# Hybrid DeltaNet and Conformer layer on one core: gates as seven half-size products ahead of the heads, branch products token-major, the mixed sum turned on TensorE

## The chip, the core and the metric

The kernel runs on one core of a Trainium2 chip. The metric is the device time of one execution in microseconds. The kernel before takes 2469.19 us, the median of 3 runs (2468.35 to 2469.48).

The engines have short names in the profile: PE is TensorE (matmul), PEld its weight load, DVE is VectorE, ACT ScalarE, POOL GpSimd, SP SyncE, which here only issues DMAs. L186 is line 186 of the kernel before.

## The reference, cut to what matters

512 tokens, 2048 channels, float32 throughout.

```
h = rmsnorm(x)
qkv, z_a, b_raw, a_raw, glu_in, z_b, gate_logits = split(h @ w_in)
o_a = gated_delta(short_conv(qkv), b_raw, a_raw)         # 16 heads, chunks of 64
y_a = (rmsnorm(o_a) * silu(z_a)) @ w_br_a                # branch A
u   = causal_depthwise_conv(glu(glu_in), 31 taps) + b_dw
y_b = (silu(layernorm(u)) * silu(z_b)) @ w_br_b          # branch B
gate_a, gate_b = split(sigmoid(gate_logits + b_gate))
mixed = (gate_a * y_a + gate_b * y_b) @ w_out
x = x + rmsnorm(mixed)
x = x + rmsnorm(sigmoid(x @ w_ple_gate) * (p @ w_ple_proj))
```

## The kernel before

**Numbers.** Every float32 factor is split into a high part, rounded to the type fp32r, and a low part, the rest. A product is three matmuls: high by high, high by low, low by high. ScalarE makes the high part of a weight piece (L127, a cast) and VectorE the low part (L128, a subtraction of two SBUF tensors). A piece is 128x512; `prep` makes two of them from one 512 KB load on SP's queue, and `next_piece` keeps three ahead in a ring of four buffers.

**Products.** `gemm_cm` (L170) makes one channel-major tile: 128 channels by 512 tokens, the weights stationary, 16 steps of the inner dimension with three matmuls each, so 48 matmuls and four pieces a tile. Its results take turns in two PSUM banks (the pool `gps`); an `evac` function empties each. z_a (in `z_phase`) and `w_out` are made another way, as seven half-size products (Strassen's scheme in Winograd's form) with 128x512 matmuls and the activations stationary: 336 matmuls for half of the 2048 columns where the plain way has 384. The sums of activations that it needs are formed once by the generator `form`, the sums of weight blocks by VectorE (the helper line L314) and by a DMA that adds (`acc`, on GpSimd's queue). For `w_out` these sums are made ahead by `presum` (L980): 160 DMAs on GpSimd's queue, 96 of them loads (L992), 64 stores (L997).

**Order.** The kernel is a list of jobs in program order. After each matmul of a job, `tick()` moves the generators that are active: the heads' chain (`group`, a step every HP = 4 matmuls), the depthwise convolutions (`dwconv`, one of their 30 VectorE steps every CP = 6), `presum`, `layer_norm`, and `mix`, which forms the sums of activations for `w_out`. The framework then puts the instructions of each engine in an order of its own: it follows the program order, but work that it takes to be ready may be put ahead into an engine's idle time. Each engine runs its list in order.

The stages, with their time in the trace:
- loading and normalising x, with the part of the layer embedding that doesn't depend on x1 (to 36 us)
- 5 gate tiles, then z_a as seven products (to 250 us), then the decay inputs
- the 16 heads in 8 groups of 2 (to 1191 us): per group 6 tiles of q, k, v, then `spawn(group)`, then 2 of the `rest` tiles (z_b and gates); after the last group 4 more rest tiles and the first GLU pair. `finish("heads")` issues what is left of the chain
- branch A (to about 1850 us): 16 tiles of `w_br_a`, among them the other 15 GLU pairs and the other gate tiles, with the convolutions on VectorE (L924: u and the running sum y both in SBUF) and `presum`. GpSimd adds up the channels for the layer norm (L930, two SBUF tensors)
- the layer norm of branch B's convolution, behind the remaining gate tiles; then 16 tiles of `w_br_b` (to 2119 us), with the `mix` steps
- `w_out`, 14 half-size products; the layer embedding's gate; the output (to 2467 us)

The gates go to DRAM (`g_dram`) and come back for branch A (L976, multiplied with the product from PSUM) and branch B (L1107, L1109).

Of the kernel before, what the change touches and what calls it, by code (L numbers as in the profile page):

```python
# [27 lines left out]
CP = 6  # L28
# [5 lines left out]
GATE_TILE0 = 113  # L34
# [5 lines left out]
V_BG = V_DW + NK * TAPS  # L40
V_BDW = V_BG + 32
# [41 lines left out]
def _body(ctx, tc, A, out):  # L83
# [31 lines left out]
    prepped = deque()  # L115

    def prep():
        if not prep_src:
            return
        src = prep_src.popleft()  # L120
        raw = rawp.tile([P, 1024], F32, tag="raw", name="raw", bufs=3)
        nc.sync.dma_start(raw, src)
        for q in range(2):
            rq = raw[:, q * T:(q + 1) * T]
            w = ring.tile([P, 1024], F32R, tag="w", name="w")
            hi, lo = w[:, 0:T], w[:, T:]
            nc.scalar.copy(hi, rq)  # L127
            nc.vector.tensor_tensor(lo, rq, hi.bitcast(F32), ALU.subtract)  # L128
            hi_lo[id(hi)] = w.rearrange("p (s c) -> p s c", s=2)
            prepped.append((hi, lo))  # L130
# [138 lines left out]
    g_dram = dram.tile([2 * NK, P, T], F32, name="g_dram")  # L269
    zb_dram = dram.tile([NK, P, T], F32, name="zb_dram")  # L270

    def gate_tile(i, src=True):
        def f(ps):
            t = slots.tile([P, T], F32, tag="s", name="gt")
            nc.scalar.activation(t, ps, AF.Sigmoid, bias=vv(V_BG + i))
            nc.sync.dma_start(g_dram[i], t)
        gemm_cm(w_in_tile(GATE_TILE0 + i) if src else None, hT, f)

    def zb_tile(i):
# [4 lines left out]
        gemm_cm(w_in_tile(ZB_TILE0 + i), hT, f)  # L284

    first_src = [w_in_tile(GATE_TILE0)[0], w_in_tile(GATE_TILE0)[1]]
# [20 lines left out]
    def z_phase():  # L307
# [49 lines left out]
        WZ = A["w_z"]  # L357
# [4 lines left out]
        def load(jp, blk, q):  # L362
            cnt["load"] += 1
            if cnt["load"] <= 4 or cnt["load"] % 5 in (2, 4):
                two = [slots.tile([P, T], F32, tag="s", name="zraw") for _ in range(2)]
                for n in range(2):
                    nc.sync.dma_start(two[n], WZ[jp, blk, q][:, n * T:(n + 1) * T])
                return two
            raw = rawp.tile([P, 1024], F32, tag="raw", name="raw", bufs=3)
            nc.sync.dma_start(raw, WZ[jp, blk, q])  # L370
            return [raw[:, 0:T], raw[:, T:]]

        def acc(t, jp, blk, q):
            nc.gpsimd.dma_start(t, WZ[jp, blk, q], accum_op=ALU.add)

# [3 lines left out]
        def e_a(jp, q):  # L379
            b11, b12 = load(jp, B11, q), load(jp, B12, q)  # L380
# [6 lines left out]
        def e_b(jp, q):  # L387
            b22, b12 = load(jp, B22, q), load(jp, B12, q)
# [6 lines left out]
        def e_c(jp, q):  # L395
            acc(tz[q], jp, B21, q)
            return [load(jp, B21, q), parts(tz[q])]

        for jp in range(2):
            for e in (e_a, e_b, e_c):  # L400
                entries.extend((e, jp, q) for q in range(4))

        def enter():
            e, jp, q = entries.popleft()
            for src in e(jp, q):
# [36 lines left out]
        def fin(tt, j, c):  # L442
# [4 lines left out]

        gen = form()
        gate_tile(0, False)
        for i in range(1, FILL):  # L450
            if i == FILL - 1:
                jobs.extend([enter, enter])
            gate_tile(i)
        spawn(gen, 7, "form")
        run_jobs()
        for jp in range(2):
            ps = run(("P1", "Q5"), stepper(gen, 2))
            s1, s5 = [], []
            for home, pr in ((s1, "P1"), (s5, "Q5")):
                for t in range(2):  # L460
                    home.append(unit_s("zsn"))
                    nc.scalar.copy(home[t], ps[pr][t])
# [7 lines left out]
            for t in range(2):  # L470
                tt_(d[t], ps["P3"][t], d[t], ALU.add)
                fin(t, 2 * jp + 1, d[t])
                tt_(s5[t], s5[t], u2[t], ALU.subtract)
                fin(2 + t, 2 * jp + 1, s5[t])
            ps = run(("P2", "Q4"))
            for t in range(2):
                tt_(s1[t], ps["P2"][t], s1[t], ALU.add)
                fin(t, 2 * jp, s1[t])
                tt_(u2[t], ps["Q4"][t], u2[t], ALU.add)
                fin(2 + t, 2 * jp, u2[t])  # L480
# [266 lines left out]
    def group(g):  # L747
# [134 lines left out]
        while scans:  # L882
            wait = None
            for s in list(scans):
# [3 lines left out]
                else:  # L888
# [3 lines left out]
    rest = deque([lambda i=i: zb_tile(i) for i in range(NK)] + [lambda i=i: gate_tile(i) for i in range(FILL, NK)]  # L892
                 + [lambda i=i: gate_tile(NK + i) for i in range(NK)])
    for g in range(NH // 2):
        pair = (2 * g, 2 * g + 1)
        for h in pair:
            gemm_cm(w_in_tile(16 + h), hT, evac_k(h))
            gemm_cm(w_in_tile(h), hT, evac_q(h))
            gemm_cm(w_in_tile(32 + h), hT, evac_v(h))
        jobs.append(lambda g=g: spawn(group(g), HP, "heads"))  # L900
        for _ in range(2):
            rest.popleft()()


# [4 lines left out]
    cpool = [slots, "s"]  # L909

# [22 lines left out]

    def evac_glu_a(i):
        def f(ps):
            u = sg_t.pop(i)
            nc.vector.tensor_tensor(u, ps, u, ALU.mult)
            spawn(dwconv(i, u), CP)
        return f

    def glu_pair(i):
        gemm_cm(w_in_tile(GLU_TILE0 + 16 + i), hT, evac_glu_b(i))
        gemm_cm(w_in_tile(GLU_TILE0 + i), hT, evac_glu_a(i))

    mixed = [None] * NK
    gate_b = [None] * NK

    for i in range(4):
        rest.popleft()()
    glu_pair(0)  # L950
    run_jobs()
    finish("heads")
    heads_ctx.close()


    s2_ctx = ExitStack()
    lop = s2_ctx.enter_context(tc.tile_pool(name="lop", bufs=LOP))
    s2 = s2_ctx.enter_context(tc.tile_pool(name="s2", bufs=40 - LOP))
    cpool[:] = [s2, "s2"]

    def low(n, name, dt=F32R):
        return lop.tile([P, T], dt, tag="lop", name=name) if n < LOP else s2.tile([P, T], dt, tag="s2", name=name)
    oT = []

    def split_oa():
        for h in range(NH):
            oh = low(2 * h, "oh")
            nc.scalar.copy(oh, o_a[h])
            ol = low(2 * h + 1, "ol")
            nc.vector.tensor_tensor(ol, o_a[h], oh.bitcast(F32), ALU.subtract)  # L970
            oT.append((oh, ol))
            yield
    spawn(split_oa(), 7, "oa")
    def evac_ya(i):
        def f(ps):
            nc.vector.tensor_tensor(mixed[i], ps, mixed[i], ALU.mult)  # L976
        return f

# [4 lines left out]

# [29 lines left out]
    def load_gate(i):  # L1013
        mixed[i] = slots.tile([P, T], F32, tag="s", name="gt")
        nc.sync.dma_start(mixed[i], g_dram[i])

    rest.popleft()()
    glu_pair(1)
    jobs.append(lambda: finish("oa"))
    for i in range(3):  # L1020
        jobs.append(lambda i=i: load_gate(i))
    jobs.append(lambda: spawn(presum(), 10, "presum"))
    nglu = 2
    for i in range(NK):
        gemm_cm(A["w_br_a"][i], oT, evac_ya(i))
        if i + 3 < NK:
            jobs.append(lambda i=i: load_gate(i + 3))
        if i + 5 < NK:
            rest.popleft()()
        if nglu < NK:  # L1030
            glu_pair(nglu)
            nglu += 1
# [5 lines left out]

    def layer_norm():
        while done[0] < NK:  # L1040
            yield
        for i in range(NK):
            u_t[i] = s2.tile([P, T], F32, tag="s2", name="ur")
            nc.sync.dma_start(u_t[i], u_dram[i])
            yield 3
        pm = lps.tile([P, T], F32, tag="l", name="mean_ps")
        mm(pm, ones, acc[0], start=True, stop=True)
        mean = low(0, "mean", F32)
        nc.vector.tensor_scalar(mean, pm, 1.0 / D, None, ALU.mult)
        acc2 = low(0, "acc2", F32)  # L1050
        for i in range(NK):
            u = u_t[i]
            nc.vector.tensor_tensor(u, u, mean, ALU.subtract)
            sq = low(0, "lsq", F32) if i else acc2
# [3 lines left out]
            yield 12  # L1058
        yield
        pvr = lps.tile([P, T], F32, tag="l", name="var_ps")  # L1060
        for tt in range(NTT):
            mm(pvr[:, tt:tt + 1], acc2[:, tt * P:(tt + 1) * P], ones[:, 0:1], start=True, stop=True)
        yield
# [4 lines left out]
        dg = low(0, "dg", F32)  # L1068
        for tt in range(NTT):
            nc.vector.tensor_scalar(dg[:, tt * P:(tt + 1) * P], ident, rst[:, tt:tt + 1], None, ALU.mult)  # L1070
        yield
        yield
        prs = lps.tile([P, T], F32, tag="l", name="rstd_ps")
        mm(prs, ones, dg, start=True, stop=True)
        rstd = low(0, "rstd", F32)
# [508 lines left out]
```

## Time and profile before

| what | before |
|---|---|
| runs, median of 3 | 2469.19 us |
| profiled execution: span from the first to the last instruction | 2467.1 us |
| instructions | 33147 |
| POOL busy | 219.0 us (9%) |
| ACT busy | 1110.7 us (45%) |
| HBM read, written | 310.90 MB, 48.23 MB |

The profiled execution's time outside the span isn't recorded; the median of the runs is 2.1 us above the span. Busy times of PE overlap: a 128x512 matmul is shown as some 0.39 us, but matmuls start every 0.23 us when nothing holds them up, so PE's cost is read from how many start in a stretch, not from the mean.

### The profile page before, as it was taken

How to read it: one execution, taken by the hardware profiler on the slowest of the kernel's cores; microseconds unless marked ns; L12 is line 12 of the kernel's file. 1: busy time of each engine (PE TensorE's matmuls, PEld its weight loads, DVE VectorE, ACT ScalarE, POOL GpSimd, SP SyncE). 2: the span in 40 equal slices, each digit the busy share in tenths (PEclk: the TensorE clock that was granted, in tenths of full speed). 3: DMA queues.
4: the chain of work that ended last, by engine and by line, in shares of the span. 5: the costliest groups of instructions: out<-in, count | busy, mean ns of one | idle time of the engine just before them, and what ended most of it. 6: DMA issues, size and time to landing. Idle time of an engine off the chain costs nothing.

```text
span 2467.1 us, 33147 instructions
## 1 busy us (share of the span) xinstructions
PE 2446.8 (99%) x12090; PEld 2014.3 (82%) x12090; DVE 1746.4 (71%) x3278; ACT 1110.7 (45%) x2181; POOL 219.0 (9%) x291
## 2 busy tenths in 40 slices
PE   8999999999999999999999999999999999999998
PEld 7888788888888888888888888888888888888886
DVE  7877767767676776766886877868976755667644
ACT  6455565565645556564422222222224723444532
POOL 0001100100000000000222322310000000000000
PEclk9999999999999999999999999999999999999999
DMA  7566432323232232223676866853353633575542
GB/s 268 171 173 187 133 110 86 99 86 99 74 103 95 82 99 86 98 69 115 181 224 179 235 204 181 239 161 111 106 185 123 210 118 109 213 234 168 196 171 77
DMA packets 131460, 361.31 MB, mean 146 GB/s; under 512 B 14816, under 2 KB 23264, under 8 KB 131296
## 3 DMA queue, kind: packets, MB, share of 16 engines
q1 hardware_dynamic: 112096, 310.94, 37.8%
q0 software_dynamic: 18048, 46.15, 8.1%
q10 hardware_dynamic: 1152, 2.10, 0.3%
q8 instruction: 95, 1.56, 0.3%
q14 instruction: 69, 0.57, 0.1%
HBM read 310.90 MB, written 48.23 MB: 146 GB/s over the span
## 4 chain that ended last, share of the span: by engine, by line
PE 96%; DVE 1%; issue 1%; DMA 1%; ACT 1%; POOL 0%; SPq 0%; DVEq 0%; POOLq 0%; ACTq 0%
PE g L186 23%; PE g L188 23%; PE g L184 23%; PE zp L434 2%; PE zp L432 2%; PE zp L433 2%; PE f L1274 2%; PE f L1273 2%; PE f L1272 2%; PE f L1438 2%; PE f L1436 2%; PE f L1437 2%; PE psB L704 1%; PE psS L710 1%; PE psA L698 1%
## 5 line engine op out<-in xcount | busy, mean ns | idle before, releaser
L186 PE MATMUL g<-hl,w 128*128 128x512 f32 x2048 | 809.2, 395 | 0.0
L188 PE MATMUL g<-hh,w 128*128 128x512 f32 x2048 | 809.0, 395 | 0.0
L184 PE MATMUL g<-hh,w 128*128 128x512 f32 x2048 | 807.5, 394 | 0.0
L127 ACT CAST w<-raw 128x512 fp32r<-128x512 f32 x716 | 438.3, 619 | 728.6 <-PE g L188 620.0
L128 DVE TENSOR_TENSOR w<-raw,w 128x512 fp32r<-128x512 f32 x716 | 504.2, 709 | 275.4 <-ACT w L127 273.0
L188 PEld LDWEIGHTS g<-hh,w 128*128 128x128 f32 x2048 | 385.1, 188 | 76.2 <-DVE w L128 2.6
L186 PEld LDWEIGHTS g<-hl,w 128*128 128x128 f32 x2048 | 385.1, 188 | 76.1 <-issue 1.6
L184 PEld LDWEIGHTS g<-hh,w 128*128 128x128 f32 x2048 | 385.2, 188 | 74.1 <-issue 0.5
L924 DVE SCALAR_TENSOR_TENSOR uc<-sg,vec,uc 128x511 f32<-128x511 f32 (+14 forms) x480 | 351.3, 734 | 14.0 <-ACT uc L921 3.9
L651 DVE SCALAR_TENSOR_TENSOR cv<-g,vec,cv 128x511 f32<-128x511 f32 x144 | 106.4, 739 | 28.5 <-ACT cv L649 27.8
L184 PE MATMUL g<-oh,w 128*128 128x512 f32 x256 | 99.6, 389 | 0.0
L186 PE MATMUL g<-ol,w 128*128 128x512 f32 x256 | 99.6, 389 | 0.0
L188 PE MATMUL g<-oh,w 128*128 128x512 f32 x256 | 99.6, 389 | 0.0
L184 PE MATMUL g<-uh,w 128*128 128x512 f32 x256 | 99.6, 389 | 0.0
L186 PE MATMUL g<-ul,w 128*128 128x512 f32 x256 | 99.6, 389 | 0.0
L188 PE MATMUL g<-uh,w 128*128 128x512 f32 x256 | 99.6, 389 | 0.0
L837 DVE TENSOR_TENSOR prod<-UT,VT 128x2 f32<-128x2 f32 (+30 forms) x248 | 87.3, 352 | 6.6
L992 POOL DMA_DIRECT2D wsum<-in_w_out x96 | 75.3, 847 | 78.1 <-issue 28.1
L1272 PE MATMUL f<-wsp,oph 128*128 128x512 f32 x192 | 75.6, 394 | 0.0
L1436 PE MATMUL f<-w,xh 128*128 128x512 f32 x192 | 75.3, 392 | 0.0
L1273 PE MATMUL f<-wsp,opl 128*128 128x512 f32 x192 | 75.3, 392 | 0.0
L1274 PE MATMUL f<-wsp,oph 128*128 128x512 f32 x192 | 75.2, 392 | 0.0
(370 smaller groups left out, 3406.6 us busy)
## 6 DMA issues: line engine op xcount, KB each, us to landing
raw<-in_w_in SPq DMA_DIRECT2D x258, 512.0 KB, 3.3
wsum<-in_w_out POOLq DMA_DIRECT2D x96, 256.0 KB, 5.8
raw<-in_w_ple_gate SPq DMA_DIRECT2D x40, 512.0 KB, 3.4
raw<-in_w_br_a SPq DMA_DIRECT2D x32, 512.0 KB, 3.8
wo_sums<-wsum POOLq DMA_DIRECT2D x64, 256.0 KB, 4.2
raw<-in_w_br_b SPq DMA_DIRECT2D x32, 512.0 KB, 3.3
raw<-in_w_z SPq DMA_DIRECT2D x22, 512.0 KB, 4.4
rw<-wo_sums SPq DMA_DIRECT2D x20, 512.0 KB, 4.2
```

What stands on the lines that cost most here:

```text
L127: nc.scalar.copy(hi, rq)
L128: nc.vector.tensor_tensor(lo, rq, hi.bitcast(F32), ALU.subtract)
L184: mm(ps, wh, rh, start=(k == 0), stop=False)
L186: mm(ps, wh, rl, start=False, stop=False)
L188: mm(ps, wl, rh, start=False, stop=(k == NK - 1))
L651: nc.vector.scalar_tensor_tensor(y[:, s:], ps[:, 0:T - s], vv(w0 + 3 - s), y[:, s:], ALU.mult, ALU.add)
L837: pin(nc.vector.tensor_tensor(pv_, um, vm, ALU.mult))
L924: nc.vector.scalar_tensor_tensor(y[:, s:], u[:, 0:T - s], vv(w0 + TAPS - 1 - s), y[:, s:], ALU.mult, ALU.add)
L1272: mm(ps, lh, wh[:, c], start=kk == 0, stop=False)
L1273: mm(ps, ll, wh[:, c], start=False, stop=False)
L1274: mm(ps, lh, wl[:, c], start=False, stop=kk == 7)
L1436: mm(ps[tt], lh, wh, start=k == 0, stop=False)
```

## The change

- **Gates.** `z_phase` runs over three weight matrices instead of one: z_a, the gates of branch A, the gates of branch B (two halves each). The bias comes as a broadcast row on ScalarE's queue and is added as the first two products leave PSUM. The 32 gate tiles are gone; the five tiles that open the stage are z_b tiles now.
- **Heads.** The rest tiles are the other 11 z_b tiles and the first 2 GLU pairs (15 tiles, so the last group gets one), and after the last group come 3 GLU pairs. `presum` starts behind the first group, a step every 13 matmuls instead of 10. `finish("heads")` comes 336 matmuls after the last `spawn(group)` instead of 384.
- **Convolutions.** One generator, `convs`, takes them one after the other, a step every 4 matmuls. It starts behind the last group. From GLU pair 5 on, u lies in PSUM (the pool `ups`, two banks); for pairs 0 to 4 it lies in SBUF as before.
- **Branch A.** `branch` makes token-major strips (512 tokens by 512 channels, four PSUM banks, the activations stationary), in 16 quarter strips of 48 matmuls. After pair 5 each of the pairs 6 to 15 is followed by one quarter strip; six are left for the layer norm. From the end of the heads to the layer norm's mean, GpSimd makes the low parts of the weight pieces (`low_part`).
- **Layer norm and branch B.** Mean and 1/std stay in PSUM. Branch B begins when two of the 16 normalised tiles are there, and `wanted` issues the rest as its steps need them. The strips come in the order 0, 2, 1, 3.
- **Mixed sum.** The sum is token-major now; `turned` brings it back to channel-major by four 128x128 transposes for each of the 16 tiles.
- **`w_out`.** Its products come in the order P1, P7 of the first half, P1 of the second, then the others.

```
-            nc.vector.tensor_tensor(lo, rq, hi.bitcast(F32), ALU.subtract)
+            low_part[0].tensor_tensor(lo, rq, hi.bitcast(F32), ALU.subtract)
...
-        for jp in range(2):
+        for grp, jp in [(g, n) for g in WZ for n in range(2)]:
+            rows = None if grp == "z" else bias_rows(grp, jp)
             ps = run(("P1", "Q5"), stepper(gen, 2))
...
-                    nc.scalar.copy(home[t], ps[pr][t])
+                    if rows:
+                        tt_(home[t], ps[pr][t], rows[n], ALU.add)
+                    else:
+                        nc.scalar.copy(home[t], ps[pr][t])
...
+    def convs():
+        while done[0] < NK:
+            if waiting:
+                yield from dwconv(*waiting.popleft())
+            else:
+                yield
...
-            u = sg_t.pop(i)
-            nc.vector.tensor_tensor(u, ps, u, ALU.mult)
-            spawn(dwconv(i, u), CP)
+            sg = sg_t.pop(i)
+            u = ups.tile([P, T], F32, tag="u", name="up") if ups else sg
+            nc.vector.tensor_tensor(u, ps, sg, ALU.mult)
+            waiting.append((i, u))
...
+        if g == 0:
+            jobs.append(lambda: spawn(presum(), 13, "presum"))
+        for _ in range(2):
+            if rest:
+                rest.popleft()()
...
+    jobs.append(lambda: spawn(convs(), CP, "convs"))
+    for i in range(2, 5):
+        glu_pair(i)
+    run_jobs()
+    finish("heads")
...
+    low_part[0] = nc.gpsimd
...
+    def branch(W, j, q, lhs, evac, side=None):
+        prep_src.extend([W[j, 2 * q], W[j, 2 * q + 1]])
+
+        def job():
+            if q == 0:
+                branch_ps[j] = [yps.tile([P, T], F32, tag="y", name="yp") for _ in range(NTT)]
+            ps = branch_ps[j]
+            for k in range(4 * q, 4 * q + 4):
+                wh, wl = next_piece()
+                if side:
+                    side(k)
+                for tt in range(NTT):
+                    b = slice(tt * P, (tt + 1) * P)
+                    lh, ll = lhs[k]
+                    mm(ps[tt], lh[:, b], wh, start=k == 0, stop=False)
...
+    glu_pair(5)
     jobs.append(lambda: finish("oa"))
+    for i in range(6, NK):
+        glu_pair(i)
+        next_ya()
...
     def layer_norm():
-        while done[0] < NK:
-            yield
         for i in range(NK):
+            while done[0] <= i:
+                yield
...
+        low_part[0] = nc.vector
+        pm = ups.tile([P, T], F32, tag="u", name="sum_ps")
         mm(pm, ones, acc[0], start=True, stop=True)
...
+            yield 6
...
+    jobs.append(lambda: spawn(norm, 4, "norm"))
+    while ya:
+        next_ya()
...
+    def turned(kk):
+        ps = gps.tile([P, T], F32, tag="g", name="tp")
+        for tt in range(NTT):
+            c = (kk % 4) * P
+            nc.tensor.transpose(ps[:, tt * P:(tt + 1) * P], mixed[tt][kk // 4][:, c:c + P], ident)
+        return ps
...
+    def wanted(k):
+        while uT[min(k + 1, NK - 1)] is None:
+            next(norm)
```

373 lines of the change are left out of this document (191 added, 182 removed).

## The prediction, put down before the change was run

> **What bounds the kernel now.** I read the page first: the busy shares, the slices, the chain that ended last.
>
> ```profile
> PE 2446.8 (99%) x12090; PEld 2014.3 (82%) x12090; DVE 1746.4 (71%) x3278; ACT 1110.7 (45%) x2181; POOL 219.0 (9%) x291
> PE   8999999999999999999999999999999999999998
> DVE  7877767767676776766886877868976755667644
> PE 96%; DVE 1%; issue 1%; DMA 1%; ACT 1%; POOL 0%; SPq 0%; DVEq 0%; POOLq 0%; ACTq 0%
> ```
>
> PE is busy in all slices but the first and the last, and the chain is PE for 96% of the span. The view of cores and PE's waits ask whether PE is slowed or waits:
>
> ```profile
> core 0: 2467.1 us, clock 0.999
> PE e_ps L216 <- ACT w L127: 6.1, 1, 6.1
> PE zp L434 <- DVE zw L314: 0.5, 1, 0.5
> PE zp L432 <- ACT zw L419: 0.2, 1, 0.2
> ```
>
> The clock is full, the one long wait is the first load, and the others are below 1.1 us each. So the time is the number of matmuls by the interval at which they start, and a change pays by taking matmuls away, as long as nothing else makes PE wait. The stretches by window give the interval; the last row is the heads' last group:
>
> ```profile
> 1200.00:1840.00 640.00, 640.00 (x2825) 529.96 (x2824) 521.06 (x755) 178.90 (x289) 128.41 (x172) 1.00 0.64 187
> 174.00:194.00 20.00, 20.00 (x89) 16.22 (x88) 16.96 (x28) 11.44 (x22) 0.60 (x1) 1.00 0.70 210
> 1084.00:1191.00 107.00, 107.00 (x635) 88.96 (x634) 67.14 (x179) 57.77 (x137) 5.22 (x6) 1.00 0.27 90
> ```
>
> Columns: length, then busy time and count of PE, PEld, DVE, ACT, POOL, then clock, DMA share and GB/s. In the first row a matmul starts every 640/2825 = 0.2265 us; a tile of 48 takes 10.9 us, a piece of 12 takes 2.72 us. All costs below are in these units.
>
> **The change part by part.** The sum is made on the profiled span, 2467.1 us. The measured median lies 2.1 us above it, and I add that at the end. About 0.2%, 5 us, is what a measurement of this kernel can tell from no change.
>
> *Gates.* Away go 32 tiles of 48, 1536 matmuls, 1536 x 0.2265 = 347.9 us. In come 4 halves of 336, 1344 matmuls. z_a is the same work twice, from its first matmul to the next stage's first:
>
> ```profile
> 93.89 0.39 PE L432 MATMUL zp<-w,hh 128*128 128x512 f32 x1
> ...
> 250.36 0.40 PE L499 MATMUL g<-hh,bw 128*64 128x512 f32 x1
> ```
>
> 156.5 us for two halves, with 0.7 us of waits and a slow restart at the start, so 155.5 us for each gate. The gain is 347.9 - 311.0 = 37 us. Ends: 43.5 us if matmuls start every 0.2265 us, 35 us at 156.5. VectorE carries 16.96 us of 20 in this stage. What was `form` there (64 operations, only in the first z_a half) is missing for the gates, and per half come 5 additions of 0.69 us (L314 among them), four instead of a ScalarE copy. The broadcast rows on ScalarE's queue stand ahead of its casts, but four pieces (5.4 us) are ready ahead. Cost nothing; without that cover 1 to 2 us a half.
>
> The Trainium skill (TensorE: Matmul & The Clock Gate, section "Wait — 56ns, not 53.3ns?") puts start to start at N/2.4 GHz and 2.5 ns, 215.7 ns for 512 columns. By it 192 matmuls fewer would be worth 41.4 us; the trace has 0.2265 and 0.231 us, and the rows decide.
>
> *Turning the sum.* 16 groups of four transposes. Such a group among matmuls:
>
> ```profile
> 36.56 0.48 PE L184 MATMUL g<-hh,w 128*128 128x512 f32 x1
> 36.88 0.60 PE L261 MATMUL xp<-cst,x 128*128 128x128 f32 x4
> 37.24 0.48 PE L186 MATMUL g<-hl,w 128*128 128x512 f32 x1
> ```
>
> From matmul to matmul 0.68 us instead of 0.2265, 0.45 us a group, 16 x 0.45 = 7.2 us more. All of it is on PE. (These rows also show a later product put between earlier transposes: the order isn't strictly the program's.)
>
> *Branch products.* Token-major or not, 768 matmuls each, 12 to a piece: nothing. At the end of a strip four banks are emptied by two VectorE operations of 0.69 us each (branch A one), while the last step's matmuls reach the four banks 0.68 us apart and the next strip needs them in the same order: nothing.
>
> *Branch A's low parts on GpSimd.* L930 is the nearest row for its cost: two SBUF tensors, 128x512.
>
> ```profile
> L128 DVE TENSOR_TENSOR w<-raw,w 128x512 fp32r<-128x512 f32 x716 | 504.2, 709 | 275.4 <-ACT w L127 273.0
> L930 POOL TENSOR_TENSOR acc<-acc,uc 128x512 f32<-128x512 f32 x15 | 19.6, 1306 | 334.0 <-DVE uc L924 334.0
> 1385.25 1.29 POOL L930 TENSOR_TENSOR acc<-acc,uc 128x512 f32<-128x512 f32 x1 [8.76 <-DVE uc L924]
> 1385.52 1.57 DVE L128 TENSOR_TENSOR w<-raw,w 128x512 fp32r<-128x512 f32 x1 [0.45 <-ACT w L127]
> 295.19 1.33 POOL L623 TENSOR_TENSOR tg<-cst,gl 128x512 fp32r<-128x512 f32 x1 [3.74 <-PE r_ps L629]
> 295.52 0.68 DVE L633 TENSOR_TENSOR E_mk<-r_ps,gc 128x512 f32<-128x512 f32 x1
> ```
>
> 1.31 us in 2.72 us: GpSimd keeps up, three pieces (8 us) ahead. But the third and fourth row show that VectorE's subtraction of two SBUF tensors, started inside GpSimd's operation, took 1.57 us and ended 0.55 us after it: it stood still until GpSimd was done. The last two rows show that an operation with one input in PSUM didn't (0.68 us). The Trainium skill (GPSIMD Engine Reference, section "8. Key points") says that GpSimd shares its SBUF interfaces with VectorE, with contention for VectorE instructions "with two SBUF inputs"; the trace agrees, 1.57 against 0.71 us. So convolutions 5 to 15, with u in PSUM, go undisturbed; what is left of 0 to 4 at the end of the heads, and the 16 subtractions of o_a, doesn't.
>
> ```profile
> L924 DVE SCALAR_TENSOR_TENSOR uc<-sg,vec,uc 128x511 f32<-128x511 f32 (+14 forms) x480 | 351.3, 734 | 14.0 <-ACT uc L921 3.9
> ```
>
> Those five have 150 steps of 0.73 us. Convolution 0 can run in the idle time of the group before (its u is ready 336 matmuls ahead). VectorE idles 107 - 67.1 = 39.9 us in the last group, 30 us of it behind the start of `convs`, room for 37 steps after three evacuations. So 150 - 30 - 37 = 83 steps remain, 60.6 us, and 16 x 0.6 us for o_a (four such operations take 2.50 us in the layer norm's row below), 70 us. VectorE gets for them 1.41 of each 2.72 us, a share of 0.52. The two `gps` banks let PE run ahead of VectorE's evacuations by one to two tiles (say 16 us). PE then runs for 86 us, VectorE does 45 us of the 70, and PE waits for the other 25. Lower end: 0, if more steps lie ahead of the heads' end. With all the idle time of the last two groups filled (71 us), 48 us remain, and with two tiles of lead PE waits for 12. I take 9, nearer the lower end: no row shows this form of operation (L924's) held up, and the packing is a guess.
>
> *`presum` in the heads.* 160 DMAs pass to GpSimd's queue, where the heads have their powers and copies, and GpSimd takes its list in order:
>
> ```profile
> L997 POOL DMA_DIRECT2D wo_sums<-wsum x64 | 39.0, 615 | 101.0 <-DMA wsum<-in_w_out 101.0
> DVE O L734 <- POOL ors L730: 18.9, 16, 1.2
> ```
>
> The stores waited 101.0 us in all for loads to land, 1.6 us each. Behind them would stand the power for o_a's norm (L730), for which VectorE already waits 1.2 us a head, and behind VectorE the chain's next matmuls. In the heads a step comes every 13 matmuls and the chain's own, 13 x 107/384 = 3.6 us against 10 x 0.2265 = 2.27 us before, so most loads have landed. I take 2 us, ends 0 and 15 (one wait of 1.6 us in each of 9 critical places would be that).
>
> *End of the heads.* 48 matmuls fewer cover the last group; its last steps get products of pair 5 put between them, as above. Nothing; 12 us if not.
>
> *Layer norm.* It loses its cover of gate tiles.
>
> ```profile
> 1857.98 2.50 DVE L1053 TENSOR_TENSOR ur<-ur,mean 128x512 f32<-128x512 f32 x4
> ...
> 1881.69 0.68 DVE L128 TENSOR_TENSOR w<-raw,w 128x512 fp32r<-128x512 f32 x1
> 1901.69 0.50 PE L1062 MATMUL var_ps<-cst,acc 128*128 128x1 f32 x4
> 1914.60 0.68 DVE L1091 TENSOR_TENSOR ul<-ur,uh 128x512 fp32r<-128x512 f32 x1
> ```
>
> The loop of squares takes 24 us, from the variance to the first normalised tile 13.6 us, some of it idle steps; I take 11. After the last GLU product come 7 quarter strips, 76 us; the last convolution 22, mean 2, loop 24, the rest 11 make 59, so VectorE's work would fit. But PE's own steps stand where the program puts them: the convolutions' last step 1984 matmuls behind the start of `convs`, branch B at 2112. The matmul for 1/std then stands 14 matmuls (3.2 us) ahead of branch B, and from it to the first tile it is some 6 of those 13.6 us, an estimate. PE waits 3 us (ends 0 and 8). In B's first strip VectorE has 4 operations of 0.6 us in 2.72 us: covered. The `w_out` order: three products (33 us) cover the last strip's turning: nothing.
>
> Sum: 2467.1 - 37.0 + 7.2 + 9 + 2 + 3 = 2451.3; with 2.1 it is **2453.4 us**.
>
> **The rivals.**
> *Slower: GpSimd shuts VectorE out.* One place, the first 100 us behind the heads; the mechanism of the 1.57 us row. It decides when PE's wait there passes 37 - 7.2 - 2 - 3 = 25 us. That is the upper end above. If the idle time of the last group takes no step at all, 120 steps and o_a's 10 us are 97 us, PE runs 113, VectorE does 59 and PE waits 38: 2453.4 - 9 + 38 = 2482. For it: an operation like the row at 1385.52 stands beside nearly every one of the 15 additions of L930. Against it: none of them is L924's. This is also the skill's rule, taken in full. Chance 0.15.
> *No waits.* Everything hides, as in the 640 us without idle PE: 2453.4 - 14 = 2439. Against it: VectorE has less slack than in those rows. 0.12.
> *GpSimd's queue holds up the heads,* 13 us more: 2466, no change. For it the 101.0 us, against it the wider steps. 0.08.
> *The seven products don't save,* VectorE becoming the bound there (16.96 of 20 us and the additions): 3 us a half, 2465. 0.05.
>
> **How the numbers follow.** My forecast has 0.60, with 2445 to 2462 as its own range. Faster by over 0.2%: the forecast and "no waits", 0.72. Slower: most of the first rival, with a little of the third, 0.14. Same: the rest, 0.14. The range goes from 2435 (no waits and gates near 0.2265 us) to 2478 (most of the first rival).
>
> **What would show it.** PE's count falls by 192 and rises by 64 transposes. The two gate groups take some 155 us each without waits. Right behind the heads, PE waits for a `gps` bank, released by a VectorE multiplication (u from ps and sg), and L924 steps there take 1.5 us or more where GpSimd's subtractions run, 0.73 us later on. A wait of a few us before branch B's first matmul. The forecast is wrong if PE waits over 25 us behind the heads, or if waits on GpSimd appear in every group.

## The result, and the profile after

The changed kernel takes **2490.6 us** (median of 4 runs, 2489.57 to 2491.45) against 2468.77 us before (4 runs, 2468.3 to 2469.48): ratio 1.0087, 95% interval 1.0073 to 1.0101. It is slower by 0.9%; 2453.4 was forecast, and the range ended at 2478. The profiled execution has a span of 2489.7 us, 22.6 us more than before.

From its page, the busy row, two rows of slices and the chain, and the view of cores:

```profile
PE 2431.6 (98%) x11962; PEld 1989.3 (80%) x11962; DVE 1821.3 (73%) x3401; ACT 1160.2 (47%) x2284; POOL 426.5 (17%) x451
PE   8999999999999999999999989799999999999998
DVE  7878787877677676777767799978777854667644
PE 32%; DVE 5%; issue 1%; ACT 0%; POOL 0%; DMA 0%; DVEq 0%; POOLq 0%; ACTq 0%; SPq 0%
```
```profile
core 0: 2489.7 us, clock 0.991
```

128 matmuls fewer, as planned, yet more time: PE is idle for 58.1 us instead of 20.3, in slices 24 and 26 above all, where VectorE stands at 9. The clock is 0.991, not 0.999. The parts of the chain do not add up to the span here (it breaks off early), so I go by PE's waits:

```profile
PE g L187 <- POOL w L127: 14.0, 1, 14.0
PE e_ps L215 <- ACT w L126: 6.3, 1, 6.3
PE py L867 <- DVE Tc L861: 4.9, 1, 4.9
PE yp L1052 <- ACT uh L1140: 4.6, 1, 4.6
PE f L1341 <- DVE sf L1225: 4.4, 1, 4.4
```

The second is the first load, as before. The other four are new and lie at four places: behind the heads, in the last group of heads, ahead of branch B, in `w_out`. The account by stages, in us (from the starts of the first matmuls of each; a group is timed between the first transposes of its second head's output; the 347.9 us are the 32 gate tiles at 0.2265 us a matmul):

| stage | before | after | difference |
|---|---|---|---|
| gates and z_a | 156.5 + 347.9 | 464.4 | -40.0 |
| group 4 of the heads | 107.5 | 108.9 | +1.4 |
| last group of the heads | 107.2 | 127.8 | +20.6 |
| heads' end to branch B (the rest of the 22.6) | | 429.0 | +22.9 |
| branch B | 174.1 | 185.0 | +10.9 |
| `w_out` to the end | 348.0 | 354.8 | +6.8 |

The windows of the two gates, the last group, and the stretch behind the heads (length; PE, PEld, DVE, ACT, POOL; clock):

```profile
250.36:404.00 153.64, 153.64 (x670) 125.25 (x669) 121.64 (x196) 73.99 (x128) 7.03 (x8) 1.00 0.68 196
404.00:558.30 154.30, 154.30 (x672) 125.75 (x671) 121.02 (x194) 76.68 (x137) 12.66 (x24) 1.00 0.65 193
1413.00:1520.00 107.00, 96.87 (x515) 75.00 (x514) 95.14 (x213) 44.08 (x93) 15.91 (x12) 0.95 0.23 74
1521.00:1635.00 114.00, 97.80 (x422) 79.88 (x421) 112.06 (x136) 34.71 (x59) 56.80 (x39) 0.94 0.38 126
```

The gates came out as planned, without a wait. In the last two rows VectorE is the full engine: 95 of 107 us (67 before), then 112 of 114.

**Last group.** Each group has a substitution in the heads' chain: on VectorE 31 pairs of a product `prod` (L846) and a reduction (L847), 62 operations, each waiting for the one before. VectorE's rows at its end in the last group; then the matmul that waits for it:

```profile
1466.21 0.76 DVE L922 SCALAR_TENSOR_TENSOR uc<-sg,vec,uc 128x492 f32<-128x492 f32 x1
1466.85 0.44 DVE L847 TENSOR_REDUCE VT<-prod 128x8 f32<-128x248 f32 x1
1467.17 0.76 DVE L922 SCALAR_TENSOR_TENSOR uc<-sg,vec,uc 128x491 f32<-128x491 f32 x1
1467.81 0.66 DVE L846 TENSOR_TENSOR prod<-UT,VT 128x256 f32<-128x256 f32 x1
```
```profile
1471.88 0.28 PE L867 MATMUL py<-Tc,W 32*32 32x32 f32 x2 [4.95 <-DVE Tc L861]
```

In these rows a convolution step (L922) stands between every two operations of the chain. The view of line L846 gives the length of the last substitution and of the one a group earlier:

```profile
L846 DVE TENSOR_TENSOR prod<-UT,VT x31: 153/332/676, 1419.2 to 1467.8; 128x2 f32<-128x2 f32 x1, 128x3 f32<-128x3 f32 x1, 128x4 f32<-128x4 f32 x1, 128x10 f32<-128x10 f32 x1
L846 DVE TENSOR_TENSOR prod<-UT,VT x31: 154/326/664, 1311.2 to 1337.7; 128x2 f32<-128x2 f32 x1, 128x3 f32<-128x3 f32 x1, 128x4 f32<-128x4 f32 x1, 128x10 f32<-128x10 f32 x1
```

48.6 us instead of 26.5; 39 steps lie inside. The 22.1 us are about what the group is longer (20.6).

**Behind the heads.** The forecast's mechanism, VectorE and GpSimd side by side:

```profile
1541.63 8.55 POOL L127 TENSOR_TENSOR w<-raw,w 128x512 fp32r<-128x512 f32 x5
1542.14 1.79 DVE L922 SCALAR_TENSOR_TENSOR uc<-sg,vec,uc 128x511 f32<-128x511 f32 x1
1543.85 1.78 DVE L1031 TENSOR_TENSOR ol<-oa,oh 128x512 fp32r<-128x512 f32 x1
1545.55 1.77 DVE L922 SCALAR_TENSOR_TENSOR uc<-sg,vec,uc 128x510 f32<-128x510 f32 x1
```

Five splits (the subtractions that make the low parts) take 8.55 us, one each 1.71 us; beside each of them stands exactly one VectorE operation, 1.8 us long instead of 0.75. The groups of L922 by their input tell who is hit:

```profile
L922 DVE SCALAR_TENSOR_TENSOR uc<-up,vec,uc 128x505 f32<-128x505 f32 (+18 forms) x330 | 233.2, 731 | 52.8 <-ACT uc L919 45.5
L922 DVE SCALAR_TENSOR_TENSOR uc<-sg,vec,uc 128x508 f32<-128x508 f32 (+20 forms) x150 | 128.2, 881 | 0.6
```

With u in PSUM (`up`) a step takes 731 ns, with u in SBUF (`sg`) 881 on the mean. The 14.0 us wait has a further link:

```profile
1577.39 21.70 DVE L922 SCALAR_TENSOR_TENSOR uc<-sg,vec,uc 128x494 f32<-128x494 f32 x29
1593.59 1.68 POOL L928 TENSOR_TENSOR acc<-acc,uc 128x512 f32<-128x512 f32 x1 [19.90 <-DVE uc L922]
1595.23 5.01 POOL L127 TENSOR_TENSOR w<-raw,w 128x512 fp32r<-128x512 f32 x3
1596.96 0.79 PE L187 MATMUL g<-hh,w 128*128 128x512 f32 x1 [14.02 <-POOL w L127]
```

VectorE works off 29 steps; GpSimd's list holds the sum of that convolution (L928) ahead of the next weight splits, so GpSimd stands still for 19.9 us, and PE waits for a split that needs nothing of VectorE.

**The clock.** After each of these four waits TensorE runs at half rate for a time. Two windows from `w_out`, right behind the wait there and 6 us later (a clock of 0.50, then 1.00):

```profile
2168.30:2171.00 2.70, 2.62 (x6) 2.15 (x7) 0.95 (x2) 0.69 (x2) 0.00 (x0) 0.50 0.00 0
2174.00:2176.00 2.00, 2.00 (x10) 1.67 (x9) 0.67 (x1) 1.75 (x2) 0.00 (x0) 1.00 0.79 260
```

From 2168.4 to 2174 a matmul starts every 0.43 us instead of 0.2265. The Trainium skill (TensorE: Matmul & The Clock Gate, section "What's actually happening") has the clock halve after an idle window of about 3.4 us and come back after about 3.4 us of work; the trace agrees in kind, with 5 to 6 us of work at half rate behind waits of 4.4 and 4.6 us. Over the four places PE is busy for 9.1, 3.4, 5.5 and 5.5 us at half clock; at 0.43 instead of 0.2265 us a matmul that is some 11 us lost, an estimate.

### The profile page after: what moved, and what is told of

Same layout as the page of the kernel before. It is cut to its first block, busy times and chain, and to the rows that moved or that the text cites. A ratio compares the mean times of both kernels' runs of the same rounds, so it can differ in the third digit from the quotient of the medians.

```text
span 2489.7 us, 33469 instructions
## 1 busy us (share of the span) xinstructions
PE 2431.6 (98%) x11962; PEld 1989.3 (80%) x11962; DVE 1821.3 (73%) x3401; ACT 1160.2 (47%) x2284; POOL 426.5 (17%) x451
## 5 line engine op out<-in xcount | busy, mean ns | idle before, releaser
L187 PE MATMUL g<-hh,w 128*128 128x512 f32 x1536 | 611.4, 398 | 16.1 <-POOL w L127 14.0
L183 PE MATMUL g<-hh,w 128*128 128x512 f32 x1536 | 610.4, 397 | 2.8 <-DVE up L943 1.6
L185 PE MATMUL g<-hl,w 128*128 128x512 f32 x1536 | 611.4, 398 | 0.0
L127 DVE TENSOR_TENSOR w<-raw,w 128x512 fp32r<-128x512 f32 x444 | 307.3, 699 | 170.6 <-ACT w L126 168.3
L187 PEld LDWEIGHTS g<-hh,w 128*128 128x128 f32 x1536 | 289.8, 189 | 73.3 <-POOL w L127 14.4
L183 PEld LDWEIGHTS g<-hh,w 128*128 128x128 f32 x1536 | 289.9, 189 | 57.9 <-ACT w L126 3.0
L922 DVE SCALAR_TENSOR_TENSOR uc<-up,vec,uc 128x505 f32<-128x505 f32 (+18 forms) x330 | 233.2, 731 | 52.8 <-ACT uc L919 45.5
L127 POOL TENSOR_TENSOR w<-raw,w 128x512 fp32r<-128x512 f32 x144 | 193.9, 1349 | 221.4 <-ACT w L126 216.2
L922 DVE SCALAR_TENSOR_TENSOR uc<-sg,vec,uc 128x508 f32<-128x508 f32 (+20 forms) x150 | 128.2, 881 | 0.6
L660 DVE SCALAR_TENSOR_TENSOR cv<-g,vec,cv 128x511 f32<-128x511 f32 x144 | 106.3, 738 | 27.3 <-ACT cv L658 26.8
L1052 PE MATMUL yp<-w,uh 128*128 128x512 f32 x256 | 101.3, 396 | 4.6 <-ACT uh L1140 4.6
L1054 PE MATMUL yp<-w,uh 128*128 128x512 f32 x256 | 101.0, 395 | 0.0
L1054 PE MATMUL yp<-w,oh 128*128 128x512 f32 x256 | 99.7, 390 | 0.5 <-POOL w L127 0.5
L1052 PE MATMUL yp<-w,oh 128*128 128x512 f32 x256 | 100.1, 391 | 0.0
L425 PE MATMUL zp<-w,zoh 128*128 128x512 f32 x256 | 99.9, 390 | 0.0
L427 PE MATMUL zp<-w,zoh 128*128 128x512 f32 x256 | 99.7, 389 | 0.0
L846 DVE TENSOR_TENSOR prod<-UT,VT 128x2 f32<-128x2 f32 (+30 forms) x248 | 87.7, 354 | 5.8
```

What stands on the lines that cost most here:

```text
L127: low_part[0].tensor_tensor(lo, rq, hi.bitcast(F32), ALU.subtract)
L183: mm(ps, wh, rh, start=(k == 0), stop=False)
L185: mm(ps, wh, rl, start=False, stop=False)
L187: mm(ps, wl, rh, start=False, stop=(k == NK - 1))
L425: mm(ps[pr][t], lh, wh, start=q + n == 0, stop=False)
L660: nc.vector.scalar_tensor_tensor(y[:, s:], ps[:, 0:T - s], vv(w0 + 3 - s), y[:, s:], ALU.mult, ALU.add)
```

## Experiments

My theory: VectorE has too much to do from the last group on, and where its convolution steps stand decides what is late. Rivals: GpSimd's list alone; GpSimd's hold on VectorE alone. "Steps ahead" counts convolution steps done by the heads' end, "behind" is the stretch from there to branch B's first matmul.

| run | us | ratio to before, 95% interval | last group, us | steps ahead | behind, us |
|---|---|---|---|---|---|
| changed kernel | 2490.6 | 1.0073-1.0101 | 127.8 | 80 | 429.0 |
| e1 | 2499.2 | 1.0107-1.0137 | 129.4 | 78 | 437.0 |
| e2 | 2493.5 | 1.0084-1.0118 | 123.7 | 75 | 433.2 |
| e3 | 2547.8 | 1.0304-1.0335 | 105.5 | 0 | 508.5 |
| e4 | 2481.8 | 1.0040-1.0070 | 124.5 | 75 | 423.8 |
| e5 | 2513.0 | 1.0159-1.0193 | 124.7 | 76 | 442.6 |
| e6 | 2495.2 | 1.0090-1.0121 | 119.4 | 72 | 429.0 |
| e7 | 2495.8 | 1.0099-1.0129 | 122.4 | 72 | 427.5 |
| e8 | 2513.5 | 1.0164-1.0194 | 121.7 | 72 | 441.9 |
| e9 | 2512.4 | 1.0163-1.0194 | 113.3 | 60 | 461.1 |
| e10 | 2485.2 | 1.0054-1.0084 | 127.7 | 80 | 428.8 |
| e11 | 2496.5 | 1.0099-1.0129 | 110.7 | 60 | 452.3 |
| e12 | 2469.0 | 0.9996-1.0015 | 109.1 | 90 | 419.3 |
| e13 | 2462.4 | 0.9962-0.9985 | 106.2 | 120 | 421.4 |
| e14 | 2456.2 | 0.9935-0.9965 | 106.8 | 150 | 413.5 |
| e15 | 2456.1 | 0.9934-0.9963 | 106.3 | 150 | 414.0 |

### Which engine, which list (e1 to e4)

**e1, the sums on VectorE.**
```
-            nc.gpsimd.tensor_copy(acc[0], y)
+            nc.vector.tensor_copy(acc[0], y)
-            nc.gpsimd.tensor_tensor(acc[0], acc[0], y, ALU.add)
+            nc.vector.tensor_tensor(acc[0], acc[0], y, ALU.add)
```


> The sum of the convolutions (L926 and L928) moves from GpSimd to VectorE, so that on GpSimd no weight split (L127) stands behind an operation that waits for VectorE; all else as in the changed kernel. Theory (VectorE has too much to do from the last group of heads on, and the queue is only where it shows): the 14.0 us wait of PE on a split of GpSimd goes, but VectorE, with 16 operations of 0.7 us more, is as late as before and PE waits for a bank that a VectorE multiplication releases: 2478 to 2492 us. Rival (the order of GpSimd's list is the loss): the 14.0 us and the half clock behind them, 6.8 us, go whole: about 2470 us. In both, the last group of heads stays at about 128 us.

2499.2 us, 8.6 more. PE's waits of this run now begin with VectorE:

```profile
PE g L183 <- DVE up L943: 20.8, 2, 14.7
```

The wait of 14.0 us on GpSimd is gone, and two on VectorE of 20.8 us together are there. The list was where the shortage showed, not the shortage; even the theory's band was too low.

**e2, all low parts on VectorE.**
```
-    low_part[0] = nc.gpsimd
```


> All low weight parts stay on VectorE. Theory (VectorE too full): no convolution step takes over 1 us any more, which gives VectorE back about 22 us (150 steps at 881 instead of 731 ns), but 144 splits of 0.71 us, 102 us, come to it, and it is busy for 95% of the stage already: PE waits for VectorE in all of branch A and the time is 2515 to 2545 us. Rival (GpSimd in any form, by its port or by its list, is the loss): the 14.0 us wait and the half clock go, VectorE keeps up: about 2470 us.

2493.5 us, as good as the changed kernel (their intervals overlap). Both were wrong: here a step with u in SBUF takes 752 ns instead of 881, and VectorE has 144 subtractions more; by the time the two about cancel.

**e3, convolutions behind the heads.**
```
-    jobs.append(lambda: spawn(convs(), CP, "convs"))
...
     spawn(split_oa(), 7, "oa")
+    spawn(convs(), 3, "convs")
```


> The convolutions start behind the heads instead of with the last group, one step every 3 matmuls instead of 4 so that they end in time. Theory: the last group takes 128 us instead of 107.6 because convolution steps stand in VectorE's list between the steps of the heads' chain; so here it takes 107 to 110 us again, and the steps that were done in it, some 70 of 0.73 us and up to 1.7 us, come behind the heads: waits of 50 us or more there, 2500 to 2535 us. Rival (the last group is late because GpSimd's list or the shorter tail of products holds it up): the last group still takes 125 us or more.

The last group takes 105.5 us, and its substitution 25.3 us instead of 48.6: the steps were what held it up.

```profile
L846 DVE TENSOR_TENSOR prod<-UT,VT x31: 154/326/659, 1417.5 to 1442.8; 128x2 f32<-128x2 f32 x1, 128x3 f32<-128x3 f32 x1, 128x4 f32<-128x4 f32 x1, 128x10 f32<-128x10 f32 x1
```

But it takes 2547.8 us in all, worse than I had allowed: 80 more steps behind the heads cost 79.5 us there.

**e4, GpSimd from pair 8 on.**
```
-    low_part[0] = nc.gpsimd
...
     for i in range(6, NK):
+        if i == 8:
+            jobs.append(lambda: low_part.__setitem__(0, nc.gpsimd))
         glu_pair(i)
```


> The low weight parts go to GpSimd only from pair 8 on, when the five convolutions with u in SBUF are done. Theory (VectorE too full; GpSimd's hold on it and 32 splits of 0.71 us, 23 us, are about the same load): no step over 1 us, no wait on GpSimd behind the heads, but PE waits for VectorE there about as long: 2480 to 2495 us. Rival (GpSimd, by its port or its list, is the loss): the 14.0 us wait and the half clock behind it go: about 2470 us or less.

2481.8 us, inside the theory's band: 8.8 us gained, where the rival wanted 20. In the profiled executions 5.2 us of it lie behind the heads and 3.3 in the last group, which got 75 steps instead of 80.

### Thinner steps (e5 to e8)

**e5.**
```
+        if g == 6:
+            jobs.append(lambda: spawn(convs(), 8, "convs"))
...
-    jobs.append(lambda: spawn(convs(), CP, "convs"))
...
     finish("heads")
+    for a in active:
+        if a[3] == "convs":
+            a[1] = CP
```


> The convolutions start one group earlier, with a step every 8 matmuls while heads are in work (some 84 steps in 672 matmuls, where the changed kernel put some 70 into its last 288), and every 4 behind the heads as before. Theory (the density of convolution steps in VectorE's list is what makes the heads' chain late, and what is left of them behind the heads is what GpSimd's weights and sums wait for): the last group takes 107 to 112 us instead of 128, fewer steps are left, the wait of 14 us shrinks, and branch B starts earlier: 2462 to 2475 us. Rival (a step of a convolution anywhere in VectorE's list makes the chain late by itself): the last two groups take some 10 us more each and nothing is gained: 2485 to 2495 us.

**e6** is e5 with e4's edit.

> As the run before it, and the low parts go to GpSimd from pair 8 on. Theory: the two losses are of two causes and their gains add up; the later start gained 8.8 us by itself (2490.6 to 2481.8): 2455 to 2465 us. Rival (with fewer steps left the two-SBUF steps end before GpSimd's splits matter): the same time as the run before it, within 3 us.

**e7** is e6 with `spawn(mix, 6, "mix")` for `10`.

> As the run before it, and the turning and mixing steps ahead of w_out come every 6 matmuls instead of 10. Theory (the 4.4 us wait in w_out is for mixing steps that stand too late in the program, and it brings 3 us of half clock with it): that wait goes, 5 to 7 us less than the run before it. Rival (the wait is for VectorE's work on the last strip, however early its steps stand): no change, within 2 us.

**e8** is e7 with no low part on GpSimd.

> As the run before it, with all low parts on VectorE. Theory (VectorE too full): 112 splits of 0.71 us more on VectorE than in the run before it, 80 us, into a stage of some 420 us in which it has 30 to 50 us idle: 10 to 30 us slower than the run before it. Rival (VectorE has the room once the steps are spread): the same time, within 4 us, so that GpSimd's part isn't needed at all.

2513.0, 2495.2, 2495.8, 2513.5 us. My theory of density fell, and the rival was too mild: in e5 the last *two* groups take 123.3 and 124.7 us, 16 and 17 us too long, and the time is 18 us above the rival's band. The order of VectorE's instructions shows why: with convolution 0 ready one group earlier, 29 of the steps of a convolution stand inside each of the two substitutions, although the program asked for one every 8 matmuls. The first of them takes 48.9 us:

```profile
L846 DVE TENSOR_TENSOR prod<-UT,VT x31: 154/328/627, 1311.9 to 1360.8; 128x2 f32<-128x2 f32 x1, 128x3 f32<-128x3 f32 x1, 128x4 f32<-128x4 f32 x1, 128x10 f32<-128x10 f32 x1
```

The scheduler that turns the program into engine lists fills the gaps between the dependent operations with whatever is ready. Place, not density, decides. e6 gains 17.8 us on e5, where 8.8 were expected, and its 2495.2 us still miss the theory's band. In the profiled executions the stretch behind the heads is 13.6 us shorter; the last two groups are 9.5 us shorter too, though the edit doesn't touch them (e5's profiled execution is 6.6 us above its median), so the gain isn't GpSimd's alone. e7 shows that `w_out`'s wait isn't for late mixing steps (4.4 us still), and e8's low parts on VectorE cost 17.7 us.

### Places (e9 to e12)

**e9.** Started as in e5; no step inside a substitution; the first step of each convolution is kept in its place in the list.
```
         owed, pace = 0.0, 2.6
+        steep[0] = True
...
+        steep[0] = False
         yield 22
...
+            if s == 1:
+                pin(step)
...
-                yield from dwconv(*waiting.popleft())
+                for _ in dwconv(*waiting.popleft()):
+                    yield
+                    while steep[0]:
+                        yield 2
...
+            jobs.append(lambda: spawn(convs(), 7, "convs"))
```


> Convolution 0 between the forward substitutions of the last two groups and convolution 1 behind the last one, 30 steps each; none inside a substitution (the first step of a convolution is kept in its place in VectorE's order); all else as in the changed kernel. Theory (the heads are late because convolution steps stand between the 62 dependent VectorE operations of a substitution, 39 of them in the changed kernel, whatever their number elsewhere): the groups take 107 to 110 us, some 18 us less; 20 steps more are left behind the heads, which costs 0 to 20 us there: 2472 to 2492 us. Rival (VectorE's total work in the group decides, wherever the steps stand): the last two groups together take at least 15 us too long.

2512.4 us, outside both forecasts: 2472 to 2492 was the theory's band. The groups fall to 113.0 and 113.3 us, not to 107 to 110 (the rival wanted 15 us too long for the two together; they are 11). But only 60 steps are ahead, and the time behind grows from 429.0 to 461.1 us. The windows of the convolution lines alone, ahead of and behind the heads' end, for the changed kernel and for e9 (length, VectorE's time in steps, their count):

```profile
560.00:1521.00 961.00, 61.73 (x80) 0.99 0.45 134
1521.00:1950.00 429.00, 299.01 (x400) 0.98 0.38 125
```
```profile
560.00:1511.80 951.80, 45.60 (x60) 0.99 0.45 135
1511.80:1972.90 461.10, 331.62 (x420) 0.95 0.37 122
```

VectorE's time in steps behind the heads grows by 32.6 us, the stage by 32.1: what isn't done ahead is paid there. Only 16.1 us of the 32.6 are the 20 steps that moved; the rest is that the steps take longer in sum (377.2 against 360.7 us), those with u in SBUF 905 ns each. So this pair alone doesn't show VectorE's total work to be the bound; e15 below bears on it.

**e10.**
```
-    banks = [0]
+    banks = [-1]
...
-            yield 6
+            yield 5
...
-        yield 12
+        yield 8
```


> Two small moves late in the kernel, apart from each other in the trace. The banks of w_out's products are numbered from one earlier, so that the third product gets no bank of the pool in which the strips are turned; the layer norm's squares come every 5 matmuls instead of 6, and the matmul for 1/std 8 instead of 12 behind. Theory (PE's 4.4 us wait in w_out is for a bank that a turned strip still holds, not for mixing work that is late): that wait goes with its half clock, 6 to 7 us. Rival (the third product's own operands are late): it stays within 1 us. For the layer norm: 20 matmuls earlier are 4.5 us; if the chain from the variance to the first tile is what branch B waits for, its 4.6 us become 0 to 2; if VectorE's work on the squares (24 us) is, they stay. All in all 2478 to 2484 us by the theory, 2488 or more by the rival.

2485.2 us, 5.4 less and just above the theory's band. `w_out` to the end takes 349.4 us instead of 354.8, and its longest wait is now another:

```profile
PE f L1341 <- ACT wsp L1322: 1.7, 1, 1.7
```

The third product had been given a bank of the pool in which the strips are turned, still held by one. Branch B's wait stayed (4.4 us), and the matmul for 1/std starts 0.9 us earlier, not 4.5: it is VectorE's work on the squares that is late.

**e11** is e9, e4 and e10 together; **e12** also moves the first GLU tiles up and starts a group earlier:
```
+    rest = deque(list(rest)[:9] + list(rest)[-4:] + list(rest)[9:-4])
...
-        if g == 6:
+        if g == 5:
```


> The three moves together: no convolution step in a substitution, low parts on GpSimd from pair 8 on, banks and layer norm as in the run before it. Theory (four separate losses that add up: heads' end 18, behind the heads 18, branch B 7, w_out 7 us): 2445 to 2460 us, below the kernel before. Rival (VectorE is short in all of branch A, and what is gained ahead is lost ahead of branch B): 2465 us or more.

> As the run before it, with the GLU products of pairs 0 and 1 put two tiles earlier among the heads' products, so that three convolutions instead of two (90 steps instead of 60) are done ahead of the heads' end, all outside the substitutions. Theory: what waits remain behind the heads come of the steps left there; 30 fewer, 22 us of VectorE, take them away: up to 5 us less than the run before it, 2440 to 2456 us. Rival (30 steps in one scan are too many, or the earlier GLU tiles cost the heads): the last groups take 112 us or more, and the time is no better.

e11: 2496.5 us, as the rival had it: with 60 steps done ahead, PE waits 16.2 us for the layer norm's squares.

```profile
PE var_ps L1130 <- DVE acc L1126: 16.2, 1, 16.2
```

e12, with 90 ahead: 2469.0 us, the time of the kernel before. That is 27.5 us less than e11, where at most 5 were expected, and yet outside the theory's band. The last groups take 113.3, 113.9 and 109.1 us. Its two longest new waits are for VectorE, just behind a substitution and ahead of branch B:

```profile
PE psB L713 <- DVE VP L890: 9.8, 3, 3.5
PE yp L1064 <- DVE gt L1076: 7.2, 1, 7.2
```

### Room made (e13 to e15)

**e13.** Four convolutions ahead. The flag is lowered only ahead of the scans, the normalised tiles come every 12 matmuls.
```
+    rest[5:5] = [f for i in range(4) for f in (lambda i=i: glu_b(i), lambda i=i: glu_a(i))]
...
+        steep[0] = False
         scans = [head_scan(g, hh, G) for hh in range(2)]
...
+        if g == 3:
+            jobs.append(lambda: spawn(convs(), 6, "convs"))
```


> Four convolutions ahead of the heads' end, 30 steps to each of the groups 3 to 6, between the last additions to VP and the next substitution (their GLU products stand earlier among the heads' products); the layer norm's normalised tiles come every 12 matmuls instead of 8; the rest as in the run with three convolutions ahead. Theory (places and VectorE's room behind the heads are all of the loss): the groups take 107.6 to 110 us, the 7.2 us wait ahead of branch B (VectorE works on normalised tiles while the bank that PE wants is still full) goes, and 30 fewer steps are left behind the heads: 2440 to 2455 us. Rival (30 steps in a group always cost it 4 to 6 us): four groups lose 16 to 24 us together and the time stays at 2460 to 2470 us.

2462.4 us, in the rival's band; but the groups lose some 9 us together, not 16 to 24. It is faster than before for the first time, with 109.4 to 112.2 us for the three groups that carry 30 steps each.

**e14**: five pairs from position 3, the start at g == 2, and GpSimd's splits from the heads' end on as in the changed kernel; **e15**: e14 without them.

> All five convolutions whose u lies in SBUF are done ahead of the heads' end, 30 steps to each of the groups 2 to 6, and all low parts behind the heads are on GpSimd at once, as in the changed kernel. Theory: no convolution step takes over 1 us any more, no wait behind the heads, and VectorE has room in branch A: 2435 to 2450 us. Rival (GpSimd's low parts hold PE up by themselves, at 1.3 us an operation and behind the sums of the convolutions): waits on GpSimd behind the heads as in the changed kernel, 2460 us or more.

> As the run before it, with all low parts on VectorE. Theory (GpSimd's part is worth what VectorE's room is short of): VectorE has 330 steps of 0.71 us, the low parts of 144 weight pieces, 102 us, and some 60 us of other work in the 430 us from the heads' end to branch B, about all of it: 5 to 25 us slower than the run before it. Rival (once the five convolutions are ahead, VectorE has room for the low parts too): within 4 us of the run before it, and the move to GpSimd is worth nothing.

2456.2 and 2456.1 us, 0.5% faster than before; e14 lies between its theory (2450 at most) and its rival (2460 at least). From e14: its slices, its longest waits behind the first load, and the steps with u in SBUF:

```profile
PE   8999999999999999999999999999999999999998
```
```profile
PE po L748 <- DVE O L743: 2.5, 2, 2.0
PE yp L1068 <- DVE gt L1080: 1.8, 1, 1.8
```
```profile
L925 DVE SCALAR_TENSOR_TENSOR uc<-sg,vec,uc 128x511 f32<-128x511 f32 (+9 forms) x150 | 111.0, 740 | 1.3
```

These steps are all done before GpSimd's splits begin (740 ns each). Behind the heads, the changed kernel, e14 and e15:

```profile
1521.00:1950.00 429.00, 407.31 (x1785) 334.60 (x1783) 359.52 (x501) 128.28 (x211) 202.08 (x151) 0.98 0.38 125
```
```profile
1508.80:1922.30 413.50, 411.30 (x1814) 339.10 (x1812) 318.25 (x449) 138.41 (x225) 189.60 (x145) 1.00 0.40 133
```
```profile
1508.70:1922.70 414.00, 411.12 (x1813) 338.89 (x1811) 385.74 (x582) 138.23 (x224) 16.78 (x12) 1.00 0.40 132
```

VectorE has 318 and 386 us of work in 414: with the splits back it still fits. The rival of e15 holds: once the five convolutions are ahead, GpSimd's part is worth nothing. The first row corrects my theory: the changed kernel gave VectorE less to do in this stage than e15, 360 us, and PE waited. Not the sum of the stage was too large; the steps left over from the heads filled VectorE right behind them (112 of the first 114 us), and it had 68 us idle in the 315 us after.

## Why the prediction was wrong

**The step that failed is "End of the heads": nothing, 12 us if not.** It measured 20.6. I had counted VectorE's 39.9 us of idle time in a group as room for 37 steps at no cost. That idle time lies in the gaps of a dependent chain; 80 steps went in, 39 of them inside one substitution, and the chain ends in a matmul. e3 and e9 show it: without steps there the group takes 105.5 and 113.3 us. This step alone would have given 2474 us, still inside the range; the stretch behind the heads, branch B and `w_out`, below, brought the rest (10.9, 5.0 and 5.5 us).

**Behind the heads** I took 9 us, with ends 0 and 25. The waits are 14.0 + 1.6 and two of 0.7 and 0.5, 16.8 us, with 2 us of half clock. GpSimd's hold on VectorE came as forecast and the ends held; the size was half, and the wait that came of it was another: PE waited for a split stuck in GpSimd's list, and only 1.6 us for a `gps` bank. The share of 0.52 for VectorE didn't come out either. With both engines in step it was less, 0.75 us of work in 1.7. Over the 84 us that VectorE needed for what was left it was more, some 0.74 by my estimate (70 steps at 1.00 us instead of 0.74, 16 subtractions at 0.92 instead of 0.68), since GpSimd stood still for 19.9 us of them. I had leaned to the lower end because no row of the kernel before showed L924's form held up; the row at 1385.52 should have been taken for that form too.

**Gates**, -37 forecast, -40.0 measured: right. **Turning**, 7.2: branch B's 10.9 hold 13 of the 16 groups, 2.6 us of half clock and a wait of 0.8, which leaves 7.5 for them against 5.9: nearly right. **`presum`**, 2: one group is 1.4 us longer and the others aren't, so the size was right; that GpSimd's queue did it isn't shown. **Layer norm**, 3 (0 to 8): a wait of 4.6, right but for the half clock behind it. **`w_out`**, nothing: a wait of 4.4 us and 2.6 of half clock, for a bank that I hadn't followed; the cover of three products didn't matter.

**What no step held** is the clock: behind four waits it took some 11 us, which are spread over the terms here. By my terms the sum runs 2451.3 - 3.0 (gates) - 0.6 (`presum`) + 20.6 (last group) + 10.9 (to branch B, 22.9 against 9 + 3) + 5.0 (branch B, beside its 5.9) + 5.5 (`w_out`, beside 1.3) = 2489.7.

The slower rival named the right engine and stopped at 2482, because it priced one place of four. Its own condition, over 25 us of waiting behind the heads, wasn't met (16.8), and neither of the two signs given for a wrong forecast appeared: they looked at the wrong place. e14 comes within 3 us of the 2453.4 forecast: with VectorE's steps out of the way, the gain that the gates promised is there. What part of GpSimd's hold and what part of the load it takes off cancel in e2 isn't separated; nor is it settled why the groups that carry steps still cost 10.6 us together in e14 (groups 2 to 6 take 108.2, 110.3, 111.2, 109.5 and 109.4 us instead of 107.6).

## What to carry to other kernels

Idle time of an engine inside a dependent chain isn't room: before work is put there, look at what stands between the chain's operations, and keep the new work out by order, not by pace. Where a change takes work off TensorE, draw up the next engine's budget, and by stretches rather than whole stages: here VectorE was full for 114 us and had idle time behind them, and 386 us of work did no harm where 360 us in another order did. Price every new wait of several us at TensorE with a stretch of half clock, as it followed each of the four here.

## What was not expected of the hardware

VectorE and GpSimd, each with two SBUF inputs, ran in step for stretches: one operation of each per 1.71 us, where alone they take 0.74 and 1.31; both are slowed, and a VectorE step with one input in PSUM is not (731 ns). The Trainium skill (GPSIMD Engine Reference, section "8. Key points") names contention between GpSimd and VectorE instructions that have two SBUF inputs, and the trace agrees. The half clock behind a wait of 4.4 us lasted longer than the wait, 5.6 us of work at 0.43 us a matmul.
